# A two-layer decoder on one core: 160 slots instead of 192 for the four larger expert positions, with weights loaded and slots moving in their up projections, and a 128-slot position first

## The chip, the cores and the metric

The kernel runs on one core of a Trainium2 chip. Its time is device microseconds of one execution. Before the change, three runs took 1925.34, 1926.12 and 1929.2 us, so the median is 1926.12 us. The profile and the trace come from one further execution, with a time of its own.

## The reference: what is computed

The program is a decoder trunk of two layers over 512 tokens of width 1024 in float32. Each layer normalises x, projects it, runs four token mixers, gates and merges their outputs and adds the result to x. Then comes a feed-forward part, which in layer 0 is dense and in layer 1, the one that the change touches, is a mixture of eight experts of which each token takes two:

```python
logits = (xt @ router)
top_logit, top_idx = lax.top_k(logits, TOP_K)
gates = jax.nn.softmax(top_logit, axis=-1)
# for each expert e, on the rows assigned to it:
y = (silu(h @ w1[e]) * (h @ w3[e])) @ w2[e]      # w1, w3: 1024 x 1408, w2: 1408 x 1024
# each token: the sum of its two experts' y, each times its gate
```

512 tokens give 1024 assignments. Run as it stands with its default inputs, the reference assigns 155, 146, 135, 133, 128, 116, 113 and 98 of them to the eight experts, in falling order.

## The kernel before

**Positions and slots.** `moe_route` (L1635) counts the assignments and sorts the experts by count; "position p" is the expert of rank p. A position has a fixed number of slots, `CAP`: 192 for positions 0 to 3, 128 for 4 to 7. A loop behind the experts (`moe_rest`) treats assignments that find no slot, in blocks of 128; it runs only if there are any. The positions run in the order `PORD`, here large and small in turn: 0, 4, 1, 5, 2, 6, 3, 7. Below, B1 to B4 are the large ones and S1 to S4 the small ones, in the order in which they run.

**Numbers in two parts.** Every float32 matrix is split into a rounded part "hi" and a rest "lo", both fp32r, and a product is hi·hi + lo·hi + hi·lo. For a unit of weights that arrives by DMA in `mraw` (128x1024 at most), ScalarE copies `mhi` and VectorE subtracts to get `mlo` (`m_split`, L1785). Nine `mraw` buffers and seven `mhi`/`mlo` pairs run ahead: at the start of unit u the split of unit u+6 is issued (`m_weight`, L1795).

**A small position.** The slots are the stationary operand and the weights move, 512 columns at a time (384 in the last third of w1 and w3). Per block of 128 rows of weights that is three matmuls (`stream`, L1802). The up projections (w1, then w3, in three column groups `FQ`) leave slots on partitions, so the gated product `gm` goes through TensorE transposes (`moe_T`, L1745) to become the stationary operand of the down projection.

**A large position** has 64 slots more. They cost two further matmuls per block into `po` (the hi and lo halves of 64 slots share one stationary operand of 128 columns), a `fold` that adds the two halves, and their own `gmo` and transposes. Each large position has 36 units of weights, as a small one has.

**Preparing the next position.** `moe_prep` runs as a generator beside the current position: a one-hot `O`, four small matmuls per slot group (`mx<-V,O`) for indices and gates, an indirect DMA on POOL that gathers the rows (`xg`, in the profile `f<-xd,si`), then transposes into `hh`, `hl` and, for 64 slots, `ho`. The first position's operands are made by `moe_first` with matmuls on x itself (`mx<-uv,f`).

**What sets the order.** The instructions are issued in the order in which this Python code runs. `slot()` is called after each unit: it first runs the evacuations that are pending, then `pump()` lets generators take a step, unless the planner's own clock (`Clock`, with assumed costs per instruction) has VectorE or ScalarE more than a limit ahead of TensorE. What a generator hasn't done at the end of a position is done there at once (`finish`). Each engine runs its queue in order. The outputs leave by an indirect DMA with addition (`out_d<-y,si`), one per slot group.

Of the kernel before, what the change touches and what calls it, by code (L numbers as in the profile page):

```python
# [9 lines left out]
F = mybir.dt.float32  # L10
R = mybir.dt.float32r
# [3 lines left out]
OP = mybir.AluOpType  # L15
AX = mybir.AxisListType

D = 1024
# [13 lines left out]
CAP = [192] * 4 + [128] * 4  # L32
NREST = 3
MRAW, MSPL = 9, 7
PORD = [0, 4, 1, 5, 2, 6, 3, 7]
# [283 lines left out]
class Trunk:  # L319
# [1440 lines left out]
    def moe_units(self, e):  # L1760
# [3 lines left out]
        for f0, f1 in self.FQ:  # L1764
# [11 lines left out]
    def m_load(self, n):  # L1776
        while self.nld < min(n, len(self.units)):
# [3 lines left out]
            self.load(raw[:, 0:cols], src, "sp")  # L1781
# [20 lines left out]
    def stream(self, ps, po, x, O, w, first, last):  # L1802
# [5 lines left out]
        if O is not None:  # L1808
            if first:
                mm(po, O, hi, stop=False)  # L1810
            mm(po[0:64], O[:, 0:64], lo, start=False, stop=False)
            if not first:
                mm(po, O, hi, start=False, stop=last)

    def fold(self, po, n):

        t = self.mt("fold", [64, 512], bufs=2)[:, 0:n]
        self.a(t, po[64:128], AF.Copy)
        self.v.tensor_add(t, t, po[0:64])
        return t  # L1820
# [4 lines left out]
    def moe_new(self, name, *shape):  # L1825
        if name == "O":
            return self.mt("O", [128, 4, 192])[:, :, 0:shape[-1]]
# [3 lines left out]
    def moe_first(self, p, put):  # L1831
# [3 lines left out]
        H = [self.mt(x, [128, KC, 128], R, 2) for x in ("hh", "hl", "ho")[0:2 + (n > 128)]]  # L1835
        for k0 in range(0, KC, 2):
# [6 lines left out]
            self.split(H[0][:, sl], H[1][:, sl], ps[:, :, 0:128])  # L1843
            if n > 128:
                self.split(H[2][:, sl, 0:64], H[2][:, sl, 64:128], ps[:, :, 128:192])
# [7 lines left out]
    def moe_prep(self, p, put):  # L1853
# [6 lines left out]
        H = [self.mt(n, [128, KC, 128], R, 2) for n in ("hh", "hl")]  # L1860
        for k0 in (0, 4):
            self.moe_T(slots[0][2][:, k0 * 128:], 4, 128, H[0][:, k0:], H[1][:, k0:])
            yield
        if len(slots) > 1:
            o = self.mt("ho", [128, KC, 128], R, 2)
            for k0 in (0, 4):
                self.moe_T(slots[1][2][:, k0 * 128:], 4, 64, o[:, k0:, 0:64], o[:, k0:, 64:128])
                yield
            H.append(o)
        put.append((slots, H))  # L1870

    def moe_expert(self, slots, H, fill):
        ov = len(H) > 2
# [6 lines left out]
        r = lambda i, m=128: val(i, m, 2)  # L1880
        w = lambda i, m=128: val(i, m, 1)
        g = [self.mt(n, [128, nf, 128], R) for n in (("gh", "gl", "go") if ov else ("gh", "gl"))]
        todo = []

        def turn(f0, f1, gm, go):
            n = f1 - f0
            self.moe_T(gm, n, 128, g[0][:, f0:f1], g[1][:, f0:f1])
            if ov:
                self.moe_T(go, n, 64, g[2][:, f0:f1, 0:64], g[2][:, f0:f1, 64:128])

        def unit(blocks, ps, po, x, cols, first, last):
            wt = self.m_weight()
            for i, k in enumerate(blocks):
                sl = slice(i * cols, (i + 1) * cols)
                self.stream(ps, po, (x[0][:, k, :], x[1][:, k, :]), x[2][:, k, :] if ov else None,
                            (wt[0][:, sl], wt[1][:, sl]), first and i == 0, last and i == len(blocks) - 1)

        for q, (f0, f1) in enumerate(self.FQ):
            n = (f1 - f0) * 128
            gm = self.mt("gm", [128, 512], bufs=2)[:, 0:n]  # L1900
            go = self.mt("gmo", [64, 512], bufs=2)[:, 0:n] if ov else None
            for j in range(2):
                ps, po = self.ps("mm")[:, 0:n], self.ps("po")[:, 0:n] if ov else None
                for k in range(0, KC, self.KU):
                    unit(range(k, k + self.KU), ps, po, H, n, k == 0, k + self.KU == KC)
                    if k + self.KU < KC:
                        self.slot()

                def ev(j=j, ps=ps, po=po, gm=gm, go=go, n=n):
                    if j == 0:  # L1910
                        self.a(gm, ps, AF.Silu, scale=r(0))
                    else:
                        self.v.scalar_tensor_tensor(gm, ps, r(0), gm, op0=OP.mult, op1=OP.mult)
                    if ov:
                        t = self.fold(po, n)
                        if j == 0:
                            self.a(go, t, AF.Silu, scale=r(1, 64))
                        else:
                            self.v.scalar_tensor_tensor(go, t, r(1, 64), go, op0=OP.mult, op1=OP.mult)
# [6 lines left out]
            todo.append(lambda f0=f0, f1=f1, gm=gm, go=go: turn(f0, f1, gm, go))  # L1926
# [191 lines left out]
```

## Time and profile before

| | |
|---|---|
| median of three runs | 1926.12 us |
| the profiled execution | 1926.52 us |
| its span in the trace | 1924.7 us |
| TensorE busy (matmuls) | 1900.6 us, 99% |
| VectorE / ScalarE busy | 1279.2 us, 66% / 990.1 us, 51% |
| DMA moved | 284.54 MB |

The profile is of that one execution; 1.8 us lie outside its span. A busy share counts a matmul from its start to its modelled end, and matmuls overlap, so 99% means that there is hardly a gap and not that no time could be saved: rates are read from the distance between starts. "PE" is TensorE, "PEld" its weight loads, "DVE" VectorE, "ACT" ScalarE. In the names, `mm`, `po` and `mx` are the three groups of PSUM banks (3, 2 and 3 banks). The expert part runs from about 1381 us to the end.

### The profile page before, as it was taken

To read this page: it belongs to the slowest core of one execution; us is meant where nothing else is said; L and a number is where in the kernel's file an instruction comes from. 1 tells how busy PE (TensorE), PEld (TensorE's weight loads), DVE (VectorE), ACT (ScalarE), POOL (GpSimd) and SP (SyncE) were. 2 spreads that over 40 slices of the span, in tenths; PEclk is the share of its full clock that TensorE was granted. 3 is DMA by queue.
4 is the path that set the end of the run, shared out by engine and by line. 5 is a ranking of instruction groups with operands and counts; after the bars stand their busy time and mean duration, and the time that the engine had idled before them with its cause. 6 is when DMAs were issued, how large, how long until landed. Compare 5 with 4: busy or idle time off the path is not lost.

```text
span 1924.7 us, 26363 instructions
## 1 busy us (share of the span) xinstructions
PE 1900.6 (99%) x9660; PEld 1524.7 (79%) x9660; DVE 1279.2 (66%) x2034; ACT 990.1 (51%) x1499; POOL 120.0 (6%) x179
## 2 busy tenths in 40 slices
PE   8999999999999999999999999999999999999998
PEld 6777776688888888888778776778888888788786
DVE  6779876655653333357779876565577877769776
ACT  5653555733532232344553445654466756657665
POOL 1001100000000000001100100010201101001000
PEclk9999999999999999999999999999999999999999
DMA  5322321233233223234312321152487968969876
GB/s 191 108 69 80 102 77 44 70 128 105 93 109 99 96 91 99 96 123 136 110 53 85 99 77 61 61 181 93 159 296 240 370 218 282 338 220 332 279 226 219
DMA packets 88504, 284.54 MB, mean 148 GB/s; under 512 B 11072, under 2 KB 12736, under 8 KB 88368
## 3 DMA queue, kind: packets, MB, share of 16 engines
q1 hardware_dynamic: 78912, 254.04, 38.7%
q0 software_dynamic: 9312, 28.73, 5.6%
q8 instruction: 78, 1.28, 0.3%
q14 instruction: 58, 0.48, 0.1%
q10 hardware_dynamic: 144, 0.02, 0.0%
HBM read 266.23 MB, written 14.42 MB: 146 GB/s over the span
## 4 chain that ended last, share of the span: by engine, by line
PE 89%; ACT 4%; DVE 4%; issue 2%; DMA 1%; SPq 0%; POOL 0%; POOLq 0%; DVEq 0%; ACTq 0%
PE mm L473 69%; PE po L473 10%; PE mx L473 8%; ACT s L213 3%; DVE s L213 3%; PE mx L477 2%; DVE wlo L213 0%; ACT whi L213 0%; DMA out_d<-y,si 0%; ACT L370 0%; DMA f<-xt_d 0%; DVE mlo L213 0%; DVE uv L213 0%; ACT mhi L213 0%; SPq L349 0%
## 5 line engine op out<-in xcount | busy, mean ns | idle before, releaser
L473 PE MATMUL mm<-s,whi 128*128 128x512 f32 x3168 | 999.9, 397 | 9.1 <-ACT whi L213 5.6
L473 PEld LDWEIGHTS mm<-s,whi 128*128 128x128 f32 x3168 | 586.7, 188 | 148.3 <-issue 14.2
L473 PE MATMUL mm<-s,wlo 128*128 128x512 f32 x1584 | 618.8, 391 | 0.1
L213 ACT ACTIVATE whi<-wraw 128x512 fp32r<-128x512 f32 (+1 forms) x432 | 261.0, 619 | 212.6 <-PE mm L473 127.0
L213 DVE TENSOR_TENSOR mlo<-mraw,mhi 128x1024 fp32r<-128x1024 f32 (+2 forms) x288 | 317.4, 1130 | 78.7 <-ACT mhi L213 76.0
L213 DVE TENSOR_TENSOR wlo<-wraw,whi 128x512 fp32r<-128x512 f32 (+1 forms) x432 | 286.8, 681 | 122.7 <-ACT whi L213 121.8
L473 PEld LDWEIGHTS mm<-s,wlo 128*128 128x128 f32 x1584 | 297.7, 188 | 63.6 <-DVE wlo L213 0.7
L213 ACT ACTIVATE mhi<-mraw 128x1024 fp32r<-128x1024 f32 (+2 forms) x288 | 277.6, 986 | 105.6 <-PE po L473 73.3
L213 ACT ACTIVATE s<-s 128x512 f32<-128x512 f32 (+3 forms) x238 | 150.0, 657 | 180.9 <-DVE s L213 178.8
L213 DVE TENSOR_TENSOR s<-s,s 128x512 f32<-128x512 f32 (+19 forms) x369 | 216.2, 593 | 37.4 <-ACT s L213 27.0
L213 ACT ACTIVATE s<-mm 128x512 f32<-128x512 f32 x108 | 64.2, 594 | 213.8 <-PE mm L473 205.6
L213 DVE TENSOR_TENSOR s<-s,mm 128x512 f32<-128x512 f32 x91 | 62.1, 685 | 137.0 <-PE mm L473 110.9
L473 PE MATMUL mm<-mhi,hh 128*128 128x512 f32 (+1 forms) x384 | 146.7, 382 | 0.0
L473 PE MATMUL mm<-mhi,hl 128*128 128x512 f32 (+1 forms) x384 | 143.3, 373 | 0.0
L473 PE MATMUL mm<-mlo,hh 128*128 128x512 f32 (+1 forms) x384 | 143.0, 372 | 0.3 <-DVE mlo L213 0.3
L473 PEld LDWEIGHTS mm<-mhi,hh 128*128 128x128 f32 x384 | 72.1, 188 | 12.3
L473 PEld LDWEIGHTS mm<-mlo,hh 128*128 128x128 f32 x384 | 72.1, 188 | 11.5 <-DVE mlo L213 0.9
L473 PEld LDWEIGHTS mm<-mhi,hl 128*128 128x128 f32 x384 | 72.2, 188 | 9.6
L213 DVE SCALAR_TENSOR_TENSOR s<-s,par,s 128x512 f32<-128x512 f32 (+31 forms) x110 | 77.6, 733 | 0.4
L473 PE MATMUL po<-mlo,ho 128*64 128x512 f32 (+1 forms) x192 | 72.2, 376 | 0.0
L473 PE MATMUL po<-mhi,ho 128*128 128x512 f32 (+1 forms) x192 | 71.7, 374 | 0.0
L473 PE MATMUL mm<-mhi,gh 128*128 128x512 f32 x176 | 70.8, 402 | 0.0
(180 smaller groups left out, 1801.8 us busy)
## 6 DMA issues: line engine op xcount, KB each, us to landing
mraw<-moe_w_d SPq DMA_DIRECT2D x208, 512.0 KB, 6.0
wraw<-w_gate_d SPq DMA_DIRECT2D x64, 512.0 KB, 3.3
wraw<-ffn_w_d SPq DMA_DIRECT2D x60, 512.0 KB, 3.3
wraw<-w_in_d SPq DMA_DIRECT2D x51, 512.0 KB, 3.3
mraw<-moe_w_d SPq DMA_DIRECT2D x64, 384.0 KB, 6.0
wraw<-w_branch_d SPq DMA_DIRECT2D x32, 256.0 KB, 2.7
wraw<-w_out_d SPq DMA_DIRECT2D x10, 512.0 KB, 3.6
mraw<-moe_w_d SPq DMA_DIRECT2D x16, 256.0 KB, 4.2
```

Source lines behind the costliest of these rows:

```text
L213: return f(out, *a, **k)
L473: self.nc.tensor.matmul(out, lhsT, rhs, start=start, stop=stop)
L477: self.nc.tensor.transpose(out, in_, ident)
```

## The change

Large positions get 160 slots (`OV` = 32 beyond 128). In their up projections (`moe_up_wide`) the weights are the stationary operand and the slots move: per 128x128 block of weights, `mhi` is loaded and [hi | lo] of the slots moves (320 columns), then `mlo` is loaded and hi moves (160 columns). The results already have the hidden dimension on partitions, so their transposes go; in their place stand, per pair of blocks, copies and additions of 160 columns and a split of the product. The norm factor is applied to the gathered rows by ScalarE before their transposes, not to the results. The weight units of these stages are read as pieces of 1 KB (512 B for the last block) instead of 4 KB rows; a large position has 34 units. The down projection stays, with 32 instead of 64 slots in `po`. The order is now 4, 0, 5, 1, 6, 2, 3, 7: S1 B1 S2 B2 S3 B3 B4 S4. `hh` and `hl` have one buffer. The planner takes 107 ns for an fp32r matmul under 192 columns.

```diff
+OV = 32
+CAP = [128 + OV] * 4 + [128] * 4
-PORD = [0, 4, 1, 5, 2, 6, 3, 7]
+PORD = [4, 0, 5, 1, 6, 2, 3, 7]
...
-        self.clock.run("pe", max(n / 2.4, 27.0) if lhsT.dtype == R else max(n / 0.6, 105.0), [out], [lhsT, rhs])
+        self.clock.run("pe", max(n / 2.4, 107.0 if n < 192 else 27.0) if lhsT.dtype == R else max(n / 0.6, 105.0), [out], [lhsT, rhs])
...
+    PAIRS = [(0, 2), (2, 4), (4, 6), (6, 8), (8, 10), (10, 11)]
...
+        for f0, f1 in self.PAIRS if wide else ():
...
+                part = self.ins[w][bass.ds(e, 1), :, q0 * 1024:q1 * 1024].rearrange(
+                    "o p (k f) -> p (o k) f", k=KC)[:, :, (f0 - q0) * 128:(f1 - q0) * 128]
+                for k in range(0, KC, 8 // n):
+                    u.append((part[:, k:k + 8 // n], 1024))
...
@@ moe_prep @@
+            H = [self.mt("hw", [128, KC, 2, CAP[p]], R, 2)]
+            for _, v, xg, m in slots:
+                self.a(xg[0:m], xg[0:m], AF.Identity, scale=v[0:m, 2:3])
             yield
+            for k0 in range(0, KC, 2):
+                ps = self.ps(shape=(128, 2, CAP[p]))
+                for k in range(2):
+                    for i, (_, _, xg, m) in enumerate(slots):
+                        self.tr(ps[:, k, 128 * i:128 * i + m], xg[0:m, (k0 + k) * 128:(k0 + k + 1) * 128],
+                                self.c("ident")[0:m, 0:m])
+                self.split(H[0][:, k0:k0 + 2, 0], H[0][:, k0:k0 + 2, 1], ps)
+                if k0 % 4 == 2:
+                    yield
...
+    def moe_up_wide(self, X, g, n):
+        flat = lambda k: X[:, k].rearrange("p a s -> p (a s)")
+        for f0, f1 in self.PAIRS:
+            m = f1 - f0
+            h, u = (self.mt(x, [128, 2, 128 + OV], bufs=2)[:, 0:m, 0:n] for x in ("hg", "hu"))
+            for j in range(2):
+                acc = [self.ps(("mm", "po")[j])[:, 0:2 * n] for _ in range(m)]
+                for k0 in range(0, KC, 8 // m):
+                    hi, lo = self.m_weight()
+                    for i in range(8 // m):
+                        k = k0 + i
+                        for c, ps in enumerate(acc):
+                            sl = slice((i * m + c) * 128, (i * m + c + 1) * 128)
+                            if k == 0:
+                                self.mm(ps, hi[:, sl], flat(k), stop=False)
+                            self.mm(ps[:, 0:n], lo[:, sl], X[:, k, 0], start=False, stop=False)
+                            if k > 0:
+                                self.mm(ps, hi[:, sl], flat(k), start=False, stop=(k == KC - 1))
...
+                def ev(acc=acc, t=(h, u)[j]):
+                    for c, ps in enumerate(acc):
+                        self.a(t[:, c], ps[:, n:2 * n], AF.Copy)
+                        self.v.tensor_add(t[:, c], t[:, c], ps[:, 0:n])
+
+                def last(h=h, u=u, f0=f0, f1=f1):
+                    self.v.tensor_tensor(u, u, h, op=OP.mult)
+                    hi = g[:, f0:f1, 0:n]
+                    self.a(hi, u, AF.Copy)
+                    self.v.tensor_sub(g[:, f0:f1, 192:320], u[:, :, 0:128], hi[:, :, 0:128].bitcast(F))
+                    self.v.tensor_sub(g[:, f0:f1, 160:32 + n], u[:, :, 128:n], hi[:, :, 128:n].bitcast(F))
+                self.pending += [ev, last if j else lambda h=h: self.a(h, h, AF.Silu) and None]
+                self.slot()
```

What this does to the order is seen at three places. Up to the first position's operands the two programs have the same instructions in the same order on every engine.

First, TensorE at the end of the first large position (`gh`, `gl`, `go` or `gw` are its hidden values, `hh` and `hl` the operands of the small position that follows). Before:

```order
L473 MATMUL mm<-mhi,gh 128x512
L473 MATMUL mm<-mhi,gl 128x512
L473 MATMUL mm<-mlo,gh 128x512
L473 MATMUL po<-mlo,go 64x512
L473 MATMUL po<-mhi,go 128x512
L473 MATMUL mm<-mhi,hh 128x512
L473 MATMUL mm<-mhi,hl 128x512
```

After (`f_70` holds the gathered rows):

```order
L474 MATMUL mm<-mhi,gw 128x512 x2
L474 MATMUL mm<-mlo,gw 128x512
L474 MATMUL po<-mlo,gw 32x512
L474 MATMUL po<-mhi,gw 64x512
L478 MATMUL mx<-cst,f_70 128x128 x8
L474 MATMUL mm<-mhi,hh 128x512
L474 MATMUL mm<-mhi,hl 128x512
```

The eight transposes for the small position stood in two fours within the large position's down projection before; now they stand at its very end, right before the matmuls that need their result. The same holds for B2 and B4.

Second, ScalarE at the same place. After:

```order
L214 ACTIVATE mhi<-mraw 128x1024 x5
L214 ACTIVATE y_12400<-mm,sv_11517 128x512
L214 ACTIVATE fold<-po 32x512
L214 ACTIVATE mhi<-mraw 128x1024
L214 ACTIVATE y_12400<-mm,sv_11517 128x512
L214 ACTIVATE fold<-po 32x512
L214 ACTIVATE hh<-mx 128x512 x2
L214 ACTIVATE mhi<-mraw 128x1024 x4
```

The copies `hh` now stand behind the last weight split, the second output half `y` and its `fold`.

Third, ScalarE between B3 and B4, which now follow each other (between S1 and B1 the piece is the same without the two `fold` rows). After:

```order
L214 ACTIVATE y_15122<-mm,sv_14068 128x512
L214 ACTIVATE fold<-po 32x512
L214 ACTIVATE mhi<-mraw 128x1024
L214 ACTIVATE y_15122<-mm,sv_14068 128x512
L214 ACTIVATE fold<-po 32x512
L214 ACTIVATE f_70<-f_70,sv_15165 128x1024
L214 ACTIVATE f_70<-f_70,sv_15179 32x1024
L214 ACTIVATE hw<-mx 128x2x160 x4
L214 ACTIVATE mhi<-mraw 128x1024 x2
```

The two scalings of the gathered rows, and after them the sixteen transposes and four copies into `hw`, stand wholly behind the last output half of the position before; in S2 and S3 they stand within the down projection.

## Rows read from the trace of the kernel before

**Rows 1.** The page: the span, part 1's line of busy time by engine, and of part 2 the granted TensorE clock in 40 equal slices (tenths of full speed).
```profile
span 1924.7 us, 26363 instructions
PE 1900.6 (99%) x9660; PEld 1524.7 (79%) x9660; DVE 1279.2 (66%) x2034; ACT 990.1 (51%) x1499; POOL 120.0 (6%) x179
PEclk9999999999999999999999999999999999999999
```

**Rows 2.** Busy time by engine in stretches cut at the positions' first matmuls: B1, S1, B2 and S4. The columns are the stretch, its length, busy us of PE, PEld, DVE, ACT and POOL with instruction counts, the granted clock, the DMA engines' share and GB/s.
```profile
1392.00:1475.53 83.53, 83.25 (x407) 66.68 (x407) 60.20 (x82) 50.21 (x66) 1.66 (x2) 1.00 0.78 270
1475.53:1525.00 49.47, 49.47 (x249) 42.04 (x248) 46.87 (x57) 39.94 (x48) 7.71 (x4) 1.00 0.99 354
1525.00:1606.81 81.81, 81.81 (x394) 65.63 (x394) 54.11 (x62) 47.32 (x62) 2.96 (x2) 1.00 0.75 243
...
1869.22:1916.00 46.78, 46.44 (x221) 39.49 (x220) 38.55 (x42) 34.15 (x41) 4.29 (x2) 1.00 0.70 247
```

**Rows 3.** The chain of waits from 1370 us on, in order of time: start, length, what. These pieces are the starts of S1, S2 and S4.
```profile
1475.53 14.97 PE mm L473 x66
...
1606.81 14.97 PE mm L473 x66
...
1869.22 7.96 PE mm L473 x35
```

**Rows 4.** TensorE in order of time in S1: the first and the last of 14 matmuls of 384 columns in one run, the weight load for the matmul after that one, and the first and the last of 24 matmuls of 512 columns in one run. Columns: start us, length us, what.
```profile
1500.79 0.33 PE L473 MATMUL mm<-mhi,hh 128*128 128x384 f32 x1
...
1503.04 0.33 PE L473 MATMUL mm<-mhi,hl 128*128 128x384 f32 x1
...
1503.04 0.19 PEld L473 LDWEIGHTS mm<-mlo,hh 128*128 128x128 f32 x1
...
1508.02 0.39 PE L473 MATMUL mm<-mhi,gh 128*128 128x512 f32 x1
...
1513.27 0.39 PE L473 MATMUL mm<-mlo,gh 128*128 128x512 f32 x1
```

**Rows 5.** TensorE in order of time, runs of matmuls in one row (x7: the run up to one matmul before its end; x8: the whole run). The first two have a stationary operand of 128 columns and move only 4 columns; the third is plain float32 and moves 192.
```profile
1427.60 0.84 PE L473 MATMUL mx<-V,O 128*128 128x4 f32 x7
1427.60 0.95 PE L473 MATMUL mx<-V,O 128*128 128x4 f32 x8
1384.26 7.88 PE L473 MATMUL mx<-uv,f 128*128 128x192 f32 x47
```

**Rows 6.** TensorE in order of time around four transposes in S1's down projection.
```profile
1518.20 0.40 PE L473 MATMUL mm<-mlo,gh 128*128 128x512 f32 x1
1518.44 0.60 PE L477 MATMUL mx<-cst,f 128*128 128x128 f32 x4
1518.80 0.48 PE L473 MATMUL mm<-mhi,gh 128*128 128x512 f32 x1
1519.12 0.40 PE L473 MATMUL mm<-mhi,gl 128*128 128x512 f32 x1
```

**Rows 7.** Groups of VectorE and ScalarE instructions from 1392 us on, each shape apart: out<-in, shapes and count, then busy us, mean ns of one, and the idle time before them with what ended it.
```profile
L213 DVE TENSOR_TENSOR mlo<-mraw,mhi 128x1024 fp32r<-128x1024 f32 x207 | 245.8, 1219 | 56.8 <-ACT mhi L213 54.5 <-DMA mraw<-moe_w_d 1.2
L213 DVE TENSOR_TENSOR fold<-fold,po 64x512 f32<-64x512 f32 x24 | 16.3, 678 | 8.4 <-ACT fold L213 8.4
L213 DVE TENSOR_TENSOR hl<-mx,hh 128x512 fp32r<-128x512 f32 x14 | 9.6, 687 | 5.1 <-ACT hh L213 5.0
L213 DVE TENSOR_SCALAR y<-fold,sv 64x512 f32<-64x512 f32 x8 | 4.0, 503 | 0.3
L213 DVE TENSOR_TENSOR ho<-mx,ho 128x128 fp32r<-128x128 f32 x2 | 0.6, 292 | 0.7 <-ACT ho L213 0.7
...
L213 ACT ACTIVATE mhi<-mraw 128x1024 fp32r<-128x1024 f32 x207 | 212.9, 1057 | 64.2 <-PE po L473 48.9 <-ACT mhi L213 7.8 <-PE mm L473 3.2
L213 ACT ACTIVATE y<-mm,sv 128x512 f32<-128x512 f32 x16 | 10.8, 678 | 5.8 <-PE mm L473 5.7
L213 ACT ACTIVATE hh<-mx 128x512 fp32r<-128x512 f32 x14 | 8.4, 597 | 10.3 <-PE mx L477 10.3
L213 ACT ACTIVATE ho<-mx 128x128 fp32r<-128x128 f32 x2 | 0.6, 278 | 2.7 <-DVE hl L213 2.7
```

**Rows 8.** All engines in order of time where B1 ends and S1 begins.
```profile
1475.14 0.39 PE L473 MATMUL po<-mhi,go 128*128 128x512 f32 x1
1475.42 1.05 ACT L213 ACTIVATE mhi<-mraw 128x1024 fp32r<-128x1024 f32 x1
...
1476.49 0.69 ACT L213 ACTIVATE y<-mm,sv 128x512 f32<-128x512 f32 x1
...
1477.20 0.60 ACT L213 ACTIVATE fold<-po 64x512 f32<-64x512 f32 x1
```

**Rows 9.** DMA packets by queue: SyncE's queue from 1377.3 to 1381 us, where it carries one transfer in pieces of 512 B, and from 1390 to 1405 us, where it carries expert weights in rows of 4 KB. Packets, MB, share of the 16 engines' time.
```profile
q1 hardware_dynamic: 528, 0.26, 23.8%
...
q1 hardware_dynamic: 1702, 6.20, 102.6%
```

**Rows 10.** The first unit of expert weights in order of time: its split on ScalarE and VectorE, and the first matmul.
```profile
1389.65 1.05 ACT L213 ACTIVATE mhi<-mraw 128x1024 fp32r<-128x1024 f32 x1
...
1390.73 1.22 DVE L213 TENSOR_TENSOR mlo<-mraw,mhi 128x1024 fp32r<-128x1024 f32 x1 [0.65 <-ACT mhi L213]
...
1392.01 0.53 PE L473 MATMUL mm<-mhi,hh 128*128 128x512 f32 x1
```

More of the change, by code (lines that the diff above doesn't have):

```diff
@@ L1780, in m_load @@
             self.turn(raw, "mraw", MRAW)
-            self.load(raw[:, 0:cols], src, "sp")
+            dst = raw[:, 0:cols]
+            self.load(dst if len(src.shape) == 2 else dst.rearrange("p (k f) -> p k f", k=src.shape[1]), src, "sp")
             self.raws[self.nld] = raw
@@ L1809, in stream @@
             if first:
[L1810 to L1811 removed]
+                mm(po[0:2 * OV], O, hi, stop=False)
+            mm(po[0:OV], O[:, 0:OV], lo, start=False, stop=False)
             if not first:
[L1813 removed]
+                mm(po[0:2 * OV], O, hi, start=False, stop=last)
     def fold(self, po, n):
[L1817 to L1819 removed]
+        t = self.mt("fold", [OV, 512], bufs=2)[:, 0:n]
+        self.a(t, po[OV:2 * OV], AF.Copy)
+        self.v.tensor_add(t, t, po[0:OV])
         return t
@@ L1872, in moe_expert @@
-    def moe_expert(self, slots, H, fill):
-        ov = len(H) > 2
-        nf = DFE // 128
-        def val(i, m, f):
-            if not slots:
-                fill()
-            return slots[i][1][0:m, f:f + 1]
[L1880 to L1896, printed above, removed]
+        if len(slots) == 1:
+            H = [self.mt(n, [128, KC, 128], R) for n in ("hh", "hl")]
+            for k0 in (0, 4):
+                self.moe_T(slots[0][2][:, k0 * 128:], 4, 128, H[0][:, k0:], H[1][:, k0:])
+                yield
+        else:
+            H = [self.mt("hw", [128, KC, 2, CAP[p]], R, 2)]
+            for _, v, xg, m in slots:
+                self.a(xg[0:m], xg[0:m], AF.Identity, scale=v[0:m, 2:3])
+            yield
+            for k0 in range(0, KC, 2):
[6 more added lines that the diff above has]
+                if k0 % 4 == 2:
+                    yield
@@ L1925, in moe_expert @@
                     todo.clear()
-            todo.append(lambda f0=f0, f1=f1, gm=gm, go=go: turn(f0, f1, gm, go))
-        y = [self.mt(f"y{i}", [128, D]) for i in range(len(slots))]
+            todo.append(lambda f0=f0, f1=f1, gm=gm: turn(f0, f1, gm))
+    def moe_up_wide(self, X, g, n):
[16 more added lines that the diff above has]
+                                self.mm(ps, hi[:, sl], flat(k), start=False, stop=(k == KC - 1))
+                    if k0 + 8 // m < KC:
+                        self.slot()
[10 more added lines that the diff above has]
+                self.pending += [ev, last if j else lambda h=h: self.a(h, h, AF.Silu) and None]
+                self.slot()
@@ new lines, in m_unit, with moe_expert, val @@
+    def m_unit(self, blocks, ps, po, x, O, cols, first, last):
+        wt = self.m_weight()
+        for i, k in enumerate(blocks):
+            sl = slice(i * cols, (i + 1) * cols)
+            self.stream(ps, po, (x[0][:, k, :], x[1][:, k, :]), None if O is None else O[:, k],
+                        (wt[0][:, sl], wt[1][:, sl]), first and i == 0, last and i == len(blocks) - 1)
+    def moe_expert(self, p, slots, H, fill):
+        ov = CAP[p] > 128
+        nf = DFE // 128
+        def val(i, m, f):
+            if not slots:
+                fill()
+            return slots[i][1][0:m, f:f + 1]
+        w = lambda i, m=128: val(i, m, 1)
+        todo = []
+        if ov:
+            gw = self.mt("gw", [128, nf, 2 * (128 + OV)], R)
+            self.moe_up_wide(H[0], gw, CAP[p])
+            g, O = [gw[:, :, a:a + 128] for a in (0, 192)], gw[:, :, 128:192]
+        else:
+            g, O = [self.mt(n, [128, nf, 128], R) for n in ("gh", "gl")], None
+            self.moe_up(H, g, lambda: val(0, 128, 2), todo)
+        y = [self.mt(f"y{i}", [128, D]) for i in range(1 + ov)]
@@ L1930, in moe_expert @@
             for d, (ps, po) in enumerate(acc):
-                unit(range(f0, f1), ps, po, g, 512, i == 0, i == len(self.FB) - 1)
+                self.m_unit(range(f0, f1), ps, po, g, O, 512, i == 0, i == len(self.FB) - 1)
                 if i == len(self.FB) - 1:
@@ L1960, in moe @@
         for p in PORD[1:]:
-            self.units += self.moe_units(self.expert(p))
+            self.units += self.moe_units(self.expert(p), CAP[p] > 128)
         for i in range(4):
@@ L1977, in moe @@
                 g = self.start(self.moe_prep(PORD[i + 1], put), 0)
-            self.moe_expert(slots, H, fill)
+            self.moe_expert(p, slots, H, fill)
             self.finish(g)
```

47 lines of the change are left out of this document (17 added, 30 removed).

## The prediction

> **What bounds the kernel now.** [...] A large position takes 81.8 us and a small one 49.5, TensorE without a gap in both; VectorE is at 54.1 of 81.8 us in B2 but at 46.9 of 49.5 in S1, so a small position has almost no room on VectorE and a large one has a third [rows 2]. The chain of waits says the same: it runs over matmuls, and a pair S+B takes 1606.81 - 1475.53 = 131.3 us [rows 3]. So what a large position saves on TensorE counts in full as long as the next engine in line isn't late, and every place where TensorE waits for an operand costs in full.
>
> Up to the first position's operands the order is the same on every engine, so 1381 us of the span stay. I add up differences against the span, 1924.7 us; the profiled execution took 1926.5, and the median of the runs is 0.4 below that.
>
> **Streams of the up projections.** Distances between starts: (1513.27 - 1508.02)/23 = 0.228 us per matmul of 512 columns and (1503.04 - 1500.79)/13 = 0.173 of 384 [rows 4]. Per 128x128 block of weights a large position now uses five streams over four blocks (512) or three (384): 5 x 0.228/4 = 0.285 and 5 x 0.173/3 = 0.288 us. With 11 x 8 blocks in each of w1 and w3 that is 128 x 0.285 + 48 x 0.288 = 50.3 us.
>
> After: one matmul of 320 columns and one of 160 per block. The line through the two distances has 0.43 ns per column, which gives 0.146 us for 320 and 0.077 for 160. But each has a new stationary operand of 128 columns, and there is a row for what that costs when little moves: seven and eight matmuls that move 4 columns end 0.11 us apart (0.95 - 0.84) [rows 5]. A load can lie beside a long stream (0.146 > 0.11) but not beside a short one. I take 0.146 + 0.112 = 0.258 us, so 176 x 0.258 = 45.4 us: 4.9 less per large position, 19.6 in all. Bounds for the short one: 0.077 us if the load hides, which is 704 x 0.035 = 24.6 us better, and the rate of plain float32, (7.88 - 0.33)/46 = 0.164 us for 192 columns [rows 5], hence 0.137 for 160, which is 704 x 0.025 = 17.6 us worse. No row has an fp32r matmul under 384 columns; 0.112 is nearest to the rows with 128 stationary columns.
>
> **Transposes of the gated product.** A group of four costs TensorE 1519.12 - 1518.20 - 2 x 0.228 = 0.46 us [rows 6]. A large position loses three groups for 128 slots and three for 64; the threes and the narrow ones being cheaper, I take 2.3 us each, 9.2 in all. The copies and subtractions behind them go too, and others come: per pair of blocks four copies of 160 columns on ScalarE and four additions on VectorE (between 0.28 and 0.60, 0.29 and 0.69 us for 128 and 512 columns, so 0.31 and 0.33 [rows 7]), a Silu and a copy of 320 columns (0.4 each), a product (0.5) and two subtractions (0.65 together). With four splits of 1.06 and 1.22 us that makes 6.3 us on ScalarE and 7.4 on VectorE in the 8 x 4 x 0.258 = 8.3 us that TensorE needs per pair. It is hidden; if VectorE took 10% more it would not be.
>
> **Weights in 1 KB pieces.** A packet of 512 B took 0.238 x 16 x 3.7 us / 528 = 27 ns, one of 4 KB 1.026 x 16 x 15 us / 1702 = 145, or 161 without the short semaphore packets among them [rows 9]. On the line between, 1 KB takes 46 ns, and a unit of 512 of them on 16 engines 1.5 us (at most 1.7, from the 512 B row) where it was 1.3. A unit lasts TensorE 8 x 0.258 = 2.1 us. Hidden in the large positions; in the small ones before them, which load ahead at a share of 0.99 [rows 2], nine raw and seven split buffers stand between.
>
> **Ends of the positions.** Here the change adds waits. At the end of B1, B2 and B4 the transposes of the next small position now stand behind the last matmul, and its copies behind everything on ScalarE. From that last matmul's end T (1475.14 + 0.23 for B1): before, the weight split began at T + 0.05 and ended at T + 1.1, the second half of y ended at T + 1.8 and the fold began at T + 1.8 [rows 8]. With the same queue: fold to T + 2.4, first `hh` copy (0.60) to T + 3.0; on VectorE the fold's addition (0.68) to T + 3.2, the scaling (0.50) to T + 3.7, `hl` (0.69) to T + 4.4 [rows 7]. The second matmul of the small position needs `hl`; one of 0.23 us is done by then, so TensorE loses 4.3 us, of which 0.9 were spent on these transposes before: +3.4 each, +10.2. Behind ScalarE's queue there the next splits wait, but seven units are split ahead by then.
>
> At the end of B3 comes a large position: after the fold two scalings of 1024 columns (1.06 each, as a weight split) to T + 4.5, transposes, a copy of 320 columns, its subtraction, and the last four transposes, which need a bank back: about T + 6.8, against 0.9 before: +5.9. At the end of S1 it is the same without the fold, T + 6.2, against 2.0 for four groups within a small position before: +4.2. In S2 and S3 the scalings stand behind the gather on ScalarE's queue; the gather has some 10 us to land before, and the seven units cover a delay. Their 32-row transposes are shorter: -0.6 for both.
>
> **The start.** B1 took 83.5 us where B2 took 81.8 [rows 2], so a start without anything ahead cost 1.7. S1 uses up a unit in 6 x 0.228 = 1.37 us, and VectorE needs 1.22 for a unit besides its other work. It starts at 1390.7 [rows 10]; S4, whose first units were split before, kept it busy 38.6 us [rows 2]; seven units more (8.5) and the rest of the routing (about 2), less the folds, make 47 us and some waits for ScalarE. I expect S1's last matmul at 1442, 2.5 us over a steady small position without its preparation: +0.8.
>
> **Sum.** -19.6 - 9.2 + 10.2 + 5.9 + 4.2 - 0.6 + 0.8 = -8.3 us. The end stays, since a small position is last in both and has one scatter. 1926.5 - 8.3 = 1918.2, 0.4 less against the median: **1918 us**. Own range of this case: 1911 to 1925, from 1.5 us either way at each of the four ends and 2 at the start.
>
> **Rivals.** *The short matmuls are slow* (the other side). If an fp32r matmul of 160 columns runs at the float32 rate above, each block takes 0.283 us, as much as now, and the ends stay: 1918 + 17.6 = 1936 us. It decides from 0.130 us on (8.3/704 = 0.012 above my 0.112 takes the gain away). For it: all fp32r rows have 384 columns or more. Against it: from 512 to 384 columns the time falls with the columns [rows 4].
>
> *The load of weights hides wholly.* Each block costs its streams, 0.223 us: 1918 - 24.6 = 1893 us. For it: 320 + 160 columns have 0.223 us and two loads at 0.11 the same, so a queue of loads two deep would do. Against it: the load for the matmul behind the one at 1503.04 starts with that one, not earlier [rows 4]. [...]
>
> *VectorE or the ends take the rest of the gain.* VectorE, at 7.4 of 8.3 us per pair, enters the large position with fewer units ahead after a small one at 95%, and TensorE waits 1.5 us more in each large position and 0.5 more at each end: 1918 + 8 = 1926 us, no change. For it: rows 2's small position. Against it: large positions keep a slack of 15 us on VectorE.
>
> *The loop for the rest runs*, a block of 36 units in series for one expert: far slower, over 2000 us. The reference's counts (155 at most for 160 slots, 128 for the first of 128) exclude it unless the chip's rounding moves a token at the fifth position, which is full to the slot.
>
> **Chances.** Forecast 0.62, hidden load 0.10, slow short matmuls 0.10, VectorE or ends 0.14, the rest (DMA pieces, the loop) 0.04. A run of this kernel can tell about 0.2%, 3.9 us, from no change: faster is below 1922.3, slower above 1930. Of the forecast's own range four fifths lie below 1922; with the hidden load and a little of the third rival faster gets 0.60. Same: the upper end of the forecast and half of the third rival, 0.19. Slower: 0.21. The range goes from 1893 to 1936, the two bounds of the short matmul.
>
> **What would show it.** Right: 0.258 us from block to block in the large up projections; about 78 us from a large position's first matmul to the next small one's; gaps of TensorE of 3 to 4 us before S2, S3 and S4 that end with VectorE's `hl`, of 5 to 6 before B1 and B4 that end with `hw`; VectorE near 90% in the large up projections; landing times that don't delay a split. Wrong: a distance for 160 columns of 0.08 or 0.14 us; TensorE waiting for `mlo` within a large position; gaps at the ends under 1 us, or a granted clock below full behind them.

## The result, and the profile after

The changed kernel takes **1951.03 us** (median of four runs, 1950.73 to 1951.28) where the kernel before, four runs beside it, takes 1927.66 (1925.34 to 1932.19). The ratio is 1.0118 with a 95% interval of 1.0098 to 1.0138: slower by some 23 us, where 1918 us, 8 less than before, was predicted. The range (1893 to 1936) misses it.

The page of the kernel after; the span, the busy time of the engines and the granted clock answer to [rows 1]:

```profile
span 1949.5 us, 27192 instructions
...
PE 1892.1 (97%) x10028; PEld 1537.2 (79%) x10028; DVE 1280.4 (66%) x2112; ACT 993.3 (51%) x1561; POOL 121.8 (6%) x180
...
PEclk9999999999999999999999999999989999999899
```

TensorE is busy for 8.5 us less, yet the span is 24.8 longer, and two slices of the granted clock are below nine tenths. The stretches cut at the first matmuls answer to [rows 2], with the same columns. The first two are S1 and B1 with the transposes ahead of it:

```profile
1391.19:1447.86 56.67, 50.18 (x245) 41.53 (x245) 53.10 (x68) 45.21 (x53) 4.57 (x4) 1.00 1.03 381
1447.86:1534.97 87.11, 81.95 (x495) 71.08 (x495) 55.48 (x85) 48.49 (x79) 3.39 (x3) 0.92 0.76 240
```

and this is the pair S2 + B2, which took 131.3 us before:

```profile
1534.97:1669.23 134.26, 128.58 (x731) 110.76 (x731) 101.41 (x138) 87.42 (x125) 10.35 (x7) 0.97 0.86 276
```

The pair has 5.7 us in which TensorE does nothing (134.26 - 128.58) and a mean granted clock of 0.97; before it had neither. The list of TensorE's waits from 1385 us on (engine, banks, line and what is waited for; us in total, times, longest) was all but empty before, and now reads:

```profile
PE po L474 <- DVE hu L214: 11.8, 7, 2.7
PE mx L478 <- ACT f L214: 8.1, 4, 3.5
PE mm L474 <- ACT hh L214: 6.1, 3, 2.1
PE mm L474 <- DVE hl L214: 2.2, 3, 0.7
PE mm L474 <- ACT mhi L214: 1.9, 1, 1.9
PE mx L478 <- DVE gm L214: 1.7, 1, 1.7
```

In these rows `hu` is what comes out of `po` in the large up projections (`hg` out of `mm`), `f` the gathered rows that ScalarE scales; the first row is a matmul into a `po` bank that waits for the addition which reads this bank. The second to fourth rows are the ends of the positions, which were predicted; the last two belong to S1. The first row was not predicted: it lies within the large positions. And behind these waits the clock falls. Stretches that begin where a wait has just ended, columns as in [rows 2]; the granted clock is the number behind POOL's:

```profile
1449.00:1460.00 11.00, 11.00 (x46) 8.92 (x47) 4.80 (x7) 3.75 (x6) 0.00 (x0) 0.56 1.09 322
1503.00:1508.00 5.00, 5.00 (x20) 3.95 (x19) 3.25 (x6) 2.59 (x5) 0.00 (x0) 0.66 0.60 200
1537.00:1542.00 5.00, 5.00 (x16) 3.99 (x15) 3.66 (x4) 2.35 (x3) 0.00 (x0) 0.66 1.00 219
1636.00:1641.00 5.00, 4.94 (x22) 4.59 (x23) 2.74 (x7) 2.88 (x6) 0.00 (x0) 0.66 0.58 161
1670.00:1675.00 5.00, 4.53 (x13) 3.63 (x14) 4.11 (x5) 2.11 (x3) 0.10 (x1) 0.66 1.00 224
1804.00:1815.00 11.00, 10.25 (x42) 7.88 (x43) 4.17 (x7) 4.81 (x8) 2.48 (x2) 0.56 0.60 121
1858.00:1863.00 5.00, 5.00 (x23) 4.55 (x22) 2.72 (x6) 3.08 (x6) 0.00 (x0) 0.66 0.62 175
1892.00:1897.00 5.00, 5.00 (x15) 3.96 (x16) 2.81 (x3) 2.02 (x3) 0.00 (x0) 0.66 1.00 229
```

Microsecond by microsecond the granted clock reads 1.00 or 0.50 around these eight waits, and something between only where it changes: from 1448 us on 0.72, nine times 0.50, 0.66, and 1.00 again. A mean of 0.66 over 5 us then means that some 3.4 of them were at 0.50 ("half clock" below), 0.56 over 11 us some 9.7. TensorE is busy there almost throughout, but slower: matmuls of 512 columns start 0.43 us apart at 0.50 (1537.71 to 1539.85 us) and 0.23 at 1.00 (1541.11 to 1543.85). That is 1.9 times as long, near to the clock's two, so by estimate each row costs its length times one minus the clock: 2 x 11 x 0.44 + 6 x 5 x 0.34 = 19.9 us.

With that the whole difference can be booked. I took the starts of all of TensorE's matmuls from 1380 us on: the distance to the next start is booked to the matmul's kind, a pause of over 0.3 us beyond a matmul's end to the waits, and half of what lies in a stretch at half clock to the clock (us; the last column is the best kernel of the experiments below):

| | before | after | `e8_late` |
|---|---|---|---|
| up projections | 328.8 | 307.7 | 308.1 |
| down projections, transposes, the rest | 206.8 | 199.4 | 200.2 |
| waits | 0.0 | 32.7 | 5.4 |
| half clock | 0.0 | 20.2 | 0.0 |
| sum | 535.6 | 560.0 | 513.7 |

The work itself became 28.5 us shorter, near to the 28.8 predicted for streams and transposes of the gated product together. (In the 28.5 are also some 8 us more for the transposes of gathered rows and 3 less for the first position's operands, which the prediction has in other terms.) Waits and half clock, 53 us together, took that and 24 more.

### The profile page after: what moved, and what is told of

It is laid out like the page before. It is cut to its first block, busy times and chain, and to the rows that moved or that the text cites. A ratio compares the mean times of both kernels' runs of the same rounds, so it can differ in the third digit from the quotient of the medians.

```text
span 1949.5 us, 27192 instructions
## 1 busy us (share of the span) xinstructions
PE 1892.1 (97%) x10028; PEld 1537.2 (79%) x10028; DVE 1280.4 (66%) x2112; ACT 993.3 (51%) x1561; POOL 121.8 (6%) x180
## 5 line engine op out<-in xcount | busy, mean ns | idle before, releaser
L214 ACT ACTIVATE mhi<-mraw 128x1024 fp32r<-128x1024 f32 (+2 forms) x280 | 272.8, 1004 | 87.3 <-PE mm L474 35.5
L474 PE MATMUL po<-hw,mhi 128*128 128x320 f32 x352 | 98.2, 355 | 10.6 <-DVE hu L214 10.6
L474 PE MATMUL mm<-hw,mhi 128*128 128x320 f32 x352 | 98.4, 354 | 0.2 <-DVE hg L214 0.2
L474 PE MATMUL mm<-mhi,hh 128*128 128x512 f32 (+1 forms) x192 | 74.7, 389 | 8.0 <-ACT hh L214 6.1
L474 PE MATMUL mm<-hw,mlo 128*128 128x160 f32 x352 | 81.8, 244 | 0.0
L474 PE MATMUL po<-hw,mlo 128*128 128x160 f32 x352 | 81.6, 243 | 0.0
L474 PEld LDWEIGHTS po<-hw,mhi 128*128 128x128 f32 x352 | 68.3, 194 | 11.9 <-DVE hu L214 11.9
L474 PE MATMUL mm<-mhi,hl 128*128 128x512 f32 (+1 forms) x192 | 73.6, 383 | 2.2 <-DVE hl L214 2.2
L474 PE MATMUL mm<-mlo,hh 128*128 128x512 f32 (+1 forms) x192 | 73.8, 385 | 1.2 <-DVE mlo L214 1.2
L474 PEld LDWEIGHTS mm<-hw,mhi 128*128 128x128 f32 x352 | 68.6, 195 | 1.0 <-DVE hg L214 0.6
```

The costliest lines, as they stand in the source:

```text
L214: return f(out, *a, **k)
```

## The experiments

The theory to be tested: the gain is there, and is outweighed by (a) waits at the ends of the positions, (b) a wait for `hu` at the last block of the up projections, and (c) the granted clock, which falls behind both. The rivals are named in each expectation. The kernel before stood at 1927.05, 1928.02 and 1928.11 us (medians) beside the three sets of runs.

**Idle matmuls in the waits** (`e1_fill`). `spin(n)` issues n matmuls of 320 columns (512 in a small position) on operands that lie in SBUF anyway, into an `mx` bank that nobody reads.

```diff
+            if i + 1 < NE:
+                self.spin((14 if i == 0 else 0) if CAP[p] == 128 else 22 if i == 5 else 14)
             self.finish(g)
...
+                if j and m == 1:
+                    self.spin(16)
                 acc = [self.ps(("mm", "po")[j])[:, 0:2 * n] for _ in range(m)]
```

> The changed kernel with idle matmuls (results unread) put where TensorE waits longest: at five of the seven ends of positions and before the last accumulation of each wide up projection; no wait is taken away. Theory A (a granted clock that falls behind these waits costs 20 us beside the waits themselves): the eight half-clock stretches of together 41 us go, the gaps stay in length as matmuls, 1931 us (1927 to 1936). Rival B (the time is the waits' alone, the records of the clock only go with them): no change, 1951 us (1948 to 1955). Rival C (the clock falls for another reason, such as the denser weight loads): the half-clock stretches stay in the record, 1951 us.

Measured: 1943.66 us (1939.58 to 1945.25). In the profiled run six of the eight stretches are at full clock, and the two long ones are down to some 3.5 us at half. The first three, columns as above:

```profile
1449.00:1460.00 11.00, 11.00 (x72) 10.79 (x72) 6.66 (x9) 6.23 (x11) 0.00 (x0) 0.84 0.98 288
1500.00:1510.00 10.00, 8.84 (x43) 6.21 (x42) 7.10 (x14) 5.72 (x8) 1.02 (x1) 1.00 0.63 183
1530.00:1540.00 10.00, 9.26 (x50) 7.59 (x50) 8.72 (x12) 7.44 (x9) 2.25 (x2) 1.00 0.95 261
```

So work alone, with nothing useful in it, brings the clock back and makes the kernel faster, which excludes B and C. The amount (7 us) is under half of the 20 expected. The profiled run alone (1939.58) is 11.7 us below that of the kernel after: by the booking above the clock costs 3.4 us in it instead of 20.2, but waits and all that is neither up nor down projection, idle matmuls included, make 73.2 us where they made 68.6, since these last longer than some waits and push a wait into the down projection. The other three runs show a mean granted clock of 0.993 to 0.994 where this one has 0.996; where in them it fell was not traced. The size of (c) needed a cleaner run, below.

**The last block's accumulator** (`e2_bank`).

```diff
-                acc = [self.ps(("mm", "po")[j])[:, 0:2 * n] for _ in range(m)]
+                acc = [self.ps(("mm", "po" if m > 1 else "mm")[j])[:, 0:2 * n] for _ in range(m)]
```

> The changed kernel, with the last single block's second accumulator taken from the three mm banks and not from the two po banks; nothing else. Theory A (the 2.4 to 2.7 us gap before that accumulation is a wait for a po bank to be read out): four gaps of together 10.2 us go and with them three half-clock stretches of 3.4 us, which cost 1.7 each: 1951 - 15 = 1936 us (1933 to 1941). Rival B (VectorE is behind in this stretch and the wait only moves to the next matmul that needs something of it): TensorE waits as long for po or for gw in the first units of the down projection, 1948 to 1952 us.

Measured: 1942.46 us (1941.95 to 1945.69), between the ranges of the two. TensorE's waits:

```profile
PE mm L474 <- DVE hg L214: 7.2, 4, 1.9
...
PE po L474 <- DVE hu L214: 0.4, 2, 0.2
```

The wait for `po` is gone, and 7.2 of its 11.8 us come back one step later, for the bank of `hg` at the start of the down projection: theory A for the cause, B for a part. These waits of 1.7 to 1.9 us have no half clock behind them (1.00 from 1502 to 1512, 1634 to 1644, 1766 to 1776 and 1851 to 1861 us). Why the wait arises is seen in the kernel after, in order of time around B1's last block (start us, length us, what; in brackets the idle time before it and what ended it). ScalarE:

```profile
1498.05 1.99 ACT L214 ACTIVATE mhi<-mraw 128x1024 fp32r<-128x1024 f32 x2
1499.95 0.48 ACT L214 ACTIVATE hu<-po 128x160 f32<-128x160 f32 x2
```

VectorE:

```profile
1499.13 2.36 DVE L214 TENSOR_TENSOR mlo<-mraw,mhi 128x1024 fp32r<-128x1024 f32 x2 [1.49 <-ACT mhi L214]
1501.41 0.54 DVE L214 TENSOR_TENSOR hu<-hu,po 128x160 f32<-128x160 f32 x2
```

TensorE:

```profile
1498.26 0.34 PE L474 MATMUL mm<-hw,mhi 128*128 128x320 f32 x1
1498.44 0.24 PE L474 MATMUL mm<-hw,mlo 128*128 128x160 f32 x1
1498.52 0.35 PE L474 MATMUL mm<-hw,mhi 128*128 128x320 f32 x1
1498.70 0.23 PE L474 MATMUL mm<-hw,mlo 128*128 128x160 f32 x1
...
1498.77 0.34 PE L474 MATMUL mm<-hw,mhi 128*128 128x320 f32 x1
...
1501.78 0.41 PE L474 MATMUL po<-hw,mhi 128*128 128x320 f32 x1 [2.40 <-DVE hu L214]
```

The pair before used both `po` banks until about 1497.3. The single block's first accumulation lasts 2 us instead of 4, and then its second one wants a `po` bank. But the copies out of `po` are queued behind two splits on ScalarE (1.99 us), the additions behind two on VectorE (2.36), and the bank comes back at 1501.7. On average neither engine is full (in B1's stretch above VectorE is busy for 55.5 of 87.1 us, ScalarE for 48.5); the wait comes from what stands ahead in the queue.

**The next position prepared earlier** (`e3_prep`), and **both** (`e4_both`).

```diff
-LIMS = ([5000.0, 8000.0, 8500.0, 2500.0, 2500.0], [3500.0, 8000.0, 6500.0, 2500.0, 1500.0])
+LIMS = ([5000.0, 8000.0, 8500.0, 2500.0, 2500.0, 1e9], [3500.0, 8000.0, 6500.0, 2500.0, 1500.0, 1e9])
...
-        yield 5000.0
+        yield due
         self.moe_slots(self.moe_new, O, self.V[:, :, p, :], CAP[p], slots)
-        yield 20000.0
+        yield 15000.0
...
-                g = self.start(self.moe_prep(PORD[i + 1], put), 0)
+                g = self.start(self.moe_prep(PORD[i + 1], put, 30000.0 if CAP[p] > 128 else 5000.0), 5)
```

> The changed kernel, with the steps that prepare the next position put earlier by their due times and without the planner's limit on VectorE's lead, so that the transposes of every position stand ahead of the last matmuls of the one before it; nothing is added or left out. Theory A (the gaps at the seven ends, together 16.5 us, and the clock behind them, five stretches of together 30.7 us at half = 15.4, are the largest part of what was lost): 1951 - 31 = 1920 us (1915 to 1928). Rival B (VectorE and ScalarE have no room for this earlier, and TensorE waits as long in the middle of the positions): 1940 us or more.

> Both of the two edits before this one: single block's second accumulator from mm, next position prepared earlier. Theory A (what the wide up projections save is there in full, and was outweighed by waits and by the clock behind them): 1951 - 10 - 17 - 20 = 1904 us (1899 to 1914), 20 us below the kernel before, with the granted clock at 1.00 over the whole expert part. Rival B (new waits take their place): above 1915 us, with gaps of TensorE of over 1 us within the positions.

Measured: 1927.06 us (1924.93 to 1929.38) and 1914.86 (1914.17 to 1915.98), ratio 0.9936 (0.992 to 0.9953). Earlier preparation alone takes back the whole loss, 24 us, and the two edits together make the new scheme faster than the kernel before. `e3_prep` is 7 us above A's number, within its range. The ends are mended, and 12.4 us of waits for `hu` stay, as expected, with half clock behind three of the four long ones; what comes on top is a start of S1 at 1393.7 instead of 1391.2 us (10.2 us at half clock between 1358 and 1385, ahead of all that the edit touches), a wait of 2.6 us for `gm` in S1 with 3.4 us at half clock behind it, and 3.4 us more at half clock behind one of the waits for `hu`. `e4_both` is 11 us above A's number and just outside of its range: gaps of 1.6 to 1.9 us within the positions are there, as B has it, and S1 has 6.8 us at half clock. The largest waits are

```profile
PE mm L474 <- DVE hg L214: 6.6, 4, 1.9
PE mx L478 <- ACT f L214: 2.4, 2, 1.7
```

the bank of `hg`, and the scaled rows in S1, whose preparation now stands in the up projection where VectorE is nearly full (17.2 of 18.6 us from 1391.4 to 1410).

**The two halves of the change on the kernel before**: the order of positions alone (`e5_order`), and 160 slots alone with the weights moving as before (`e7_cap`).

```diff
-PORD = [0, 4, 1, 5, 2, 6, 3, 7]
+PORD = [4, 0, 5, 1, 6, 2, 3, 7]
```
```diff
-CAP = [192] * 4 + [128] * 4
+OV = 32
+CAP = [128 + OV] * 4 + [128] * 4
...
-            mm(po[0:64], O[:, 0:64], lo, start=False, stop=False)
+            mm(po[0:OV], O[:, 0:OV], lo, start=False, stop=False)
```

> The kernel before with the order of positions alone changed (a 128-slot position first, then as in the changed kernel); slots and up projections as before. Theory A (of the new order's cost the start and the end of the first position, whose successor's 16 transposes stand behind its last matmul, are the part): first position 2 us longer, a gap of 2 to 4 us behind it and 2 to 5 us for a granted clock that falls there: 1934 us (1930 to 1939). Rival B (the order costs nothing by itself, all gaps come from the wide up projections and from the planner's view of them): 1927 us (1924 to 1930).

> The kernel before with 160 slots in the larger positions in place of 192 and nothing else: the weights still move past the slots. Theory A (a matmul costs what its moving columns cost, and there are as many as before): 1926 us (1922 to 1929). Rival B (a 64-column stationary operand in place of 128 saves time in each of the 2 x 176 matmuls of the extra slots per large position, or 32-row transposes do): 1918 us or less.

Measured: 1934.42 us for the order (ratio 1.0033, 1.0023 to 1.0044), 1925.97 for the slots (0.9988, 0.9978 to 0.9998); both as theory A has it. The order costs 6.4 us: in the profiled run by 5.0 of waits (1.8 before B1's transposes, 1.7 for `gm` in S1, 1.2 for `mlo`) and 1.7 of half clock behind S1 (0.72 from 1448 to 1454 us). Fewer slots are worth some 2 us as long as the weights move; the rest of the gain comes with turning the operands round. Whether it would come with 192 slots too was not run.

**Two more waits taken away**: the down projection's second accumulator from the `mx` banks (`e6_mx`), and, on top, the second position's preparation out of S1's up projection (`e8_late`).

```diff
-        acc = [(self.ps("mm"), self.ps("po") if ov else None) for _ in range(2)]
+        acc = [(self.ps("mx" if ov and d else "mm"), self.ps("po") if ov else None) for d in range(2)]
```
```diff
-30000.0 if CAP[p] > 128 else 5000.0), 5)
+30000.0 if CAP[p] > 128 else 5000.0 if i else 25000.0), 5)
```

> The kernel with both edits, and the second accumulator of a large position's down projection taken from the mx banks, so that it doesn't wait for the bank of hg. Theory A (the four gaps of 1.6 to 1.9 us at the start of the down projections are that bank's): 6.6 us less, 1914.9 - 6.6 = 1908 us (1905 to 1912). Rival B (VectorE is behind there in any case and TensorE waits for po or for the transposes' bank instead): 1913 us or more.

> The one before this, and the preparation of the second position 20 us later, from the first position's up projection (where VectorE is at nearly full) into its down projection. Theory A (the waits of 2.4 us for the scaled rows and of 1 us for gm in the first position come from what this preparation adds to VectorE and ScalarE there): 3 to 4 us less than the one before this, 1905 us (1901 to 1908). Rival B (the first position is bound by VectorE's total of work): the same as the one before this within 2 us.

Measured: 1908.73 us (1908.15 to 1910.32) and **1905.60** (1905.06 to 1906.42), ratios 0.9901 (0.988 to 0.9921) and 0.9883 (0.9863 to 0.9904). Both times are as A expects. In `e8_late`, though, A's reason is only a part: the wait for the scaled rows (0.7 us) is gone and that for `gm` is 1.7 us instead of 2.7, but others are longer, and TensorE's waits of over 0.3 us make 5.4 us in all against 4.7. What went is the half clock in S1, some 2 x 1.7 us, which `e6_mx` has behind each of the two waits and `e8_late` nowhere there:

```profile
1413.00:1418.00 5.00, 4.56 (x15) 3.84 (x16) 5.00 (x7) 1.38 (x3) 2.06 (x2) 0.66 0.93 314
1423.00:1428.00 5.00, 5.00 (x19) 4.65 (x20) 5.00 (x8) 4.14 (x7) 0.00 (x0) 0.66 0.84 294
```
```profile
1409.00:1429.00 20.00, 17.60 (x102) 15.93 (x102) 19.86 (x27) 16.07 (x20) 2.46 (x3) 1.00 1.00 362
```

The pair S2 + B2 of `e8_late`, first matmul to first matmul:

```profile
1521.09:1645.41 124.32, 124.16 (x732) 107.92 (x731) 100.22 (x138) 86.77 (x125) 10.50 (x6) 1.00 0.92 298
```

TensorE has hardly a gap (0.16 us) and a full clock, and the pair takes 7.0 us less than the 131.3 before. This is close to the gain that the prediction computed, 4.9 + 2.3 = 7.2 per large position, and it shows only when the waits that the new form brings are gone.

**The price of the clock by itself**: the best kernel with a wait put at the end of each large position (`e9_wait`), and the same wait with idle matmuls ahead of it (`e10_filled`).

```diff
+            if CAP[p] > 128:
+                self.slot()
+                self.spin(16)
+                self.tr(self.ps()[:, 0:OV], self.y1[0:OV, 512:640], self.c("ident")[0:OV, 0:OV])
             self.finish(g)
```

(`e9_wait` is without the `spin` line.)

> The last kernel (which has no wait at the ends of its positions), with a wait put on purpose at the end of each of the four large positions: TensorE transposes 32 rows of y1, which ScalarE and VectorE write some 3.4 us after the last matmul (copy of y, fold, addition, scaling); nothing hangs on the transposed rows. Theory A (a wait of some 3 us brings the granted clock down behind it, and that costs beside the wait): 4 x 3.4 = 13.6 us of waits and 4 stretches at half clock of 3.4 to 10 us, 1.7 to 5 each: 1905.6 + 13.6 + 12 = 1931 us (1925 to 1939). Rival B (only the wait costs): 1919 us (1916 to 1922).

> The same wait at the same four places, and 16 matmuls of 320 columns with unread results (2.3 us) ahead of each, on TensorE alone: what TensorE waits for comes at the same time. Theory A: the stretches at half clock behind the four waits don't appear, and the time is the waits' alone, 1919 us (1916 to 1922), some 7 to 20 us below the kernel without these matmuls. Rival B: the same time as without them, within 2 us.

Measured: 1926.53 us (1924.63 to 1928.97) and 1920.20 (1919.26 to 1922.87). TensorE's waits for `y` in `e9_wait` (us in total, times, longest), and three of the four stretches around them:

```profile
PE mx L478 <- DVE y L214: 14.6, 4, 3.7
```
```profile
1520.00:1535.00 15.00, 11.34 (x44) 8.80 (x42) 10.28 (x12) 9.32 (x13) 3.93 (x2) 0.77 0.85 229
1650.00:1665.00 15.00, 11.34 (x47) 8.66 (x45) 10.26 (x12) 10.11 (x13) 1.87 (x1) 0.89 0.86 238
...
1860.00:1875.00 15.00, 11.34 (x44) 8.41 (x43) 10.01 (x11) 8.85 (x12) 1.88 (x1) 0.89 0.87 243
```

The same two views of `e10_filled`:

```profile
PE mx L478 <- DVE y L214: 5.3, 4, 1.3
```
```profile
1520.00:1535.00 15.00, 13.68 (x76) 11.51 (x75) 12.21 (x17) 10.47 (x13) 3.01 (x2) 1.00 0.89 252
1650.00:1665.00 15.00, 13.68 (x77) 11.68 (x76) 12.62 (x20) 10.18 (x12) 4.46 (x3) 1.00 0.91 258
...
1860.00:1875.00 15.00, 13.69 (x64) 11.24 (x63) 12.04 (x12) 10.89 (x13) 4.25 (x2) 1.00 0.92 262
```

Both lie in A's ranges and outside B's; the difference is 6.3 us, a little under the 7 that A had as the least. With the idle matmuls the 14.6 us of waiting cost what they last: 1905.6 + 14.6 = 1920.2. Without them the same waits cost 6.3 us more (by the clock column of `e9_wait`, 15 x (0.23 + 3 x 0.11) = 8.4 in the profiled run, of which 0.8 lie within the first wait itself). So a wait of 3.7 us cost 5.2 here, and what it cost beyond its length is the clock.

## Why the prediction was wrong, point by point

- **Streams of the up projections, -19.6: right.** From block to block it is 0.257 us (the matmuls of 320 columns above start at 1498.26, 1498.52 and 1498.77), against 0.258 predicted, and the up projections lost 21.1 us. The sum is right by luck, for the parts are otherwise: 0.18 us from the long matmul to the short one and 0.07 to 0.08 from there to the next, not 0.146 and 0.112. Behind the short one the distance is that of its columns (0.077), as the rival of the hidden load has it; behind the long one it is 0.03 more than its columns, and why is not shown. (That the short matmul decides from 0.130 us on is a slip: 0.112 + 0.012 is 0.124.)
- **Transposes, -9.2, and weights in 1 KB pieces, 0: right in sum and sign.** By the booking above the transposes of the gated product went from 14.1 to 3.9 us, and no wait of TensorE is put down to a DMA. (The short packets among the 1702 of [rows 9] are 188 of under 512 B; what they carry no row shows.) S2 and S3, predicted at -0.6, did not gain: each has two groups of eight transposes for the large position that follows, half of them of 32 rows, and a group costs 1.67 us from its start to the next matmul's, where before four groups of four cost 0.35 to 0.39 each. That is 3.7 us more for both. TensorE in S2:

```profile
1577.01 1.74 PE L478 MATMUL mx<-cst,f 128*128 128x128 f32 x8
...
1578.68 0.50 PE L474 MATMUL mm<-mhi,gh 128*128 128x512 f32 x1
```

- **"It is hidden; if VectorE took 10% more it would not be": wrong.** The step compared VectorE's 7.4 us with TensorE's 8.3 per pair of blocks, an average, and that one was even too high: VectorE is busy for 111.0 of 152 us within the four up projections (1460 to 1498, 1592 to 1630, 1726 to 1764 and 1814 to 1852 us), 73% and not near 90. It passed over the last block, which is alone and half as long, and asked for a `po` bank before the queues of ScalarE and VectorE had come to it. Price: 10.2 us in four waits and 1.2 in the down projection behind them.
- **Ends of the positions, +20.3: right as waits.** From the end T of B1's last matmul the operand `hl` was to be there at T + 4.4; the matmul that needs it starts at 1536.21, 4.3 us after T (1531.65 + 0.23). TensorE in order of time there:

```profile
1531.65 0.39 PE L474 MATMUL po<-mhi,gw 128*64 128x512 f32 x1
...
1534.97 0.49 PE L474 MATMUL mm<-mhi,hh 128*128 128x512 f32 x1 [2.05 <-ACT hh L214]
1536.21 0.50 PE L474 MATMUL mm<-mhi,hl 128*128 128x512 f32 x1 [0.74 <-DVE hl L214]
```

  From S1 to B1 the first matmul came 9.5 us after T instead of 6.2, from B3 to B4 9.3 instead of 6.8; some 2.4 and 2.6 of these are half clock. The waits there end with the scaled rows (3.5 and 0.7 us from S1 to B1), not with `hw`.
- **The clock, not priced: the step that failed most.** The prediction added up every wait at its own length, and named "a granted clock below full behind them" only as a sign that it would be wrong. The trace of before couldn't show it in the expert part, where TensorE's longest wait is 0.3 us. It shows it once earlier, though, where a slice of 48 us in [rows 1] still reads 9:

```profile
334.19 0.72 PE L473 MATMUL mm<-s,whi 128*128 128x512 f32 x2 [2.39 <-DVE s L213]
```
```profile
335.00:340.00 5.00, 5.00 (x46) 3.12 (x46) 4.25 (x7) 1.60 (x4) 0.00 (x0) 0.66 0.30 106
```

  That row had the price of a wait of 2.4 us: 1.7 us more at half clock. With this behind each of the five ends to which the prediction gives a wait, its sum would by estimate have been -8.3 + 8.5 = +0.2 us, no gain. In the kernel after, behind eight of the nine waits of over 2 us at the ends and last blocks it fell to 0.50, which cost 20.2 us. `e9_wait` and `e10_filled` agree, with 6.3 us for four waits for VectorE, though not each wait did it in the kernel after.
- **The start, +0.8:** S1's last matmul starts at 1443.96, not at 1442, and `e5_order` shows that the order alone costs 6.4 us with what follows S1, where 0.8 + 4.2 were predicted and the clock was not.

Put together: -8.3 predicted, + 20.2 for the clock, + 11.4 for the `hu` wait, + 2 at the start, + 4.3 in S2 and S3, - 2.5 that the streams and the transposes of the gated product gained more = +27, against 24.8 measured between the spans. The 2 us between the two sums were not traced further. So two steps failed: the clock behind the waits, left at nothing, and the wait for `hu`, held to be hidden. Of the rivals, "VectorE or the ends take the rest of the gain" had the right place, a wait for VectorE in each large position, but another mechanism (fewer units split ahead, where no wait for `mlo` within a large position is seen) and 8 us where 33 were to be explained.

What stays open: which wait is followed by half clock, and for how long. The one of 2.70 us at 1767.66 in B3 was not (1.00 from 1767 to 1787 us), the ones of 2.40, 2.69 and 2.44 in the other large positions were. Four of 1.7 to 1.9 us among large matmuls in `e2_bank` were not, one of 1.8 us among transposes in `e5_order` was, and so was one of 0.7 us ahead of transposes in `e6_mx`. The two long stretches of the kernel after lie where sixteen transposes follow the wait, and at just these two places `e1_fill` keeps one of 3.4 us; whether the transposes have a part in it, no run here separates. And between 1358 and 1385 us, ahead of all that the change touches, some profiled runs have short stretches at half clock (`e3_prep` 10.2 us) and others none (the kernels before and after, 1.00).

## What to carry to other kernels

A gain on an engine that never waits is worth its size only while that engine goes on never waiting: price each new wait at its length and the slower work behind it, here 5.2 us for 3.7. A resource that is free on average can be late at an odd-sized last piece; look at what stands ahead of its release in each queue at that place. And a kernel whose order comes from a planner must have the planner's due times set anew with the form of the work: here a few due times, one lifted limit and two choices of banks were the difference between +23 and -22 us.

## What the runs showed of the hardware that was not expected

- An alternation of fp32r matmuls of 320 and 160 columns, each with a new stationary operand of 128 columns, runs at 0.257 us per pair; the distance behind the long one (0.18) is more than the 0.15 that its columns cost by [rows 4], and behind the short one (0.07) less than the 0.11 of [rows 5].
- Matmuls whose results nobody reads made a kernel faster: by 7.4 us in `e1_fill`, and by 6.3 in `e10_filled`, where TensorE goes on after each wait no earlier than without them (at 1525.25 us against 1524.91 behind the first) and only the granted clock differs (1.00 against 0.77 to 0.89).
- The granted clock fell to 0.50 behind most waits of 2 to 3.7 us for VectorE or ScalarE, for 3.4 us at most places and for 6.8 or 10.2 at the others.
